# Hybrid attention layer on one core: group A in rounds of two query tiles, later va projections, a fixed order for ScalarE's counts and evictions

## The chip, the core and the metric

The kernel runs as one program on one core of a Trainium2 chip. The metric is the device time of one execution in microseconds (us). Before the change the median of three runs is 1526.25 us (1521.85 to 1529.15).

## The reference

One decoder layer for 1024 tokens of width 1024, batch 1, in float32:

```
h    = rmsnorm(x) * (1 + sc1) + sh1            # sh1, sc1, ga1, sh2, sc2, ga2: silu(c) @ w_ada + b_ada
proj = h @ w_in  ->  qa, ka, va, qb, ckv, qi, ki, wi
out_a = dilated_mixture(qa, ka, va)            # 8 heads of 64, windows (128,1), (512,4), (2048,16)
score[t, s] = sum_h wi[t, h] * relu(qi[t, h] . ki[s])    # 8 index heads, causal
idx   = top_k(score, 256)                      # per query
out_b = softmax attention over the picked rows of the latent ckv (8 heads)
x = x + ga1 * (concat(out_a, out_b) @ w_out)
x = x + ga2 * ((silu(gate) * up) @ w_down)     # gate, up = modulated rmsnorm(x) @ w_gu
return rmsnorm(x)
```

In group A a query sees the keys of its own and of the preceding 128-token tile (near), and keys at strides of 4 and 16 (far). The three branches are merged by their softmax denominators.

## The kernel before

The layer runs as a row of stages: the first norm, the index projections and the index scores (to about 193 us of the profiled execution), the projections beside the top-k search (193 to 410), attention of group A (410 to 551), attention of group B (551 to 705), the output projection, the feed-forward part and the last norm. Products that must be exact in float32 are three matmuls of high and low halves (L367 to L369 for 128x512 or 128x256 results, L377 for the near scores of a head).

Each engine runs its queue in order, and that queue is put in order by a scheduler when the program is built; `tc.issue_after(x)` adds a rule to it, that what is issued inside stands behind x on its engine. SP, ACT and POOL issue DMAs, in the order of their queues too.

Modulation (`modulation`, L328 on) is eight steps, one for each half of sc2, sh2, ga1 and ga2. A step loads 2 MB of w_ada in four DMAs into a ring of three places that lies in the tile `va` (L339), has eight matmuls (L342), a copy into `sm` on ScalarE (L343) and a second small product (L347 or L351). All eight are written ahead of the first index scores (`mod(8)`, L473).

The projections are a Python generator (`projections`, L537). It has va first: two weight blocks of 8 results of 128x256 each, evicted by ScalarE (L518). Then come six weight blocks, two each of kind a (queries of group A), k (its keys) and b (queries of group B). A block is four results of 128x512; ScalarE evicts each (L499) and so frees its PSUM bank (there are five), GpSimd splits it into halves (L503, L504), and SP stores n32, nh and nl to DRAM (L506, L509). The weights come by SP (L209) and are split by GpSimd (L214, L215).

The top-k search (`chain`, L649) looks bit by bit for the 256th largest score of each of the query tiles 2 to 7. It is two searches of 16 steps. A step counts three tiles on VectorE (L626) and three on ScalarE (Sign with a sum, L629), then VectorE joins the counts (L632, L634) to the next threshold. Between the searches VectorE builds a second key (L645 to L659). The loop at L674 on interleaves both: each `yield` of the chain allows so many units of projection (1.3 a step), a 128x512 result is two units, a 128x256 result one. A step of the chain stands behind the last eviction issued (`issue_after(ev.ins)`).

After the searches `pick` (L695) turns the thresholds of a tile into a mask, on VectorE alone; tiles 7, 6 and 5 ahead of group A, tiles 2 and 3 in its second head pair, tile 4 in its third. `table` (L721, L722) builds a bias table from `tab`, which an ACT DMA loads (L548).

Group A (`attend_a`, L867) has four head pairs, each with two halves of four query tiles. For every tile and head: near scores (three matmuls, L377), far scores (L891, eight small matmuls for the two heads), VectorE adds the bias and takes the row minimum (L896), ScalarE takes the exponential (L898), TensorE transposes (L910), ScalarE and VectorE evict (L920, L922), TensorE multiplies by the values (L935, and L946 for the far blocks at the end of a half). PSUM has four banks for scores, three for transposes, one for outputs. `staged(..., 0, 0)` (L993) writes the tiles one after the other, and the scheduler interleaves TensorE's instructions. The far operands q32 and k32 are loaded for every head pair (L972, L973).

## Time and profile before

| | us |
|---|---|
| median of three runs | 1526.25 |
| profiled execution | 1529.23 |
| its span in the trace | 1527.5 |
| index stage ends, projections begin on TensorE | 193 |
| keys of the search ready on VectorE | 208 |
| first search step's counts complete | 240.8 |
| group A begins on VectorE | 410.4 |
| group B begins | 551.4 |

The tables of lines give busy time and the mean of one instruction, then the idle time of the engine just ahead of it and what ended it. The chain of waits is followed back from the last instruction of the program.

### The profile page before, as it was taken

What the parts mean: (1) busy time and instruction counts of PE and PEld (TensorE: products, weight loads), DVE (VectorE), ACT (ScalarE), POOL (GpSimd) and SP (SyncE); (2) the same over time, 40 slices, a digit from 0 to 9 for tenths busy, and PEclk for the clock granted to TensorE, in tenths of its full rate; (3) what the DMA queues carried; (4) which work ended last, traced back from release to release, by engine and by line L of the source; (5) the groups of instructions that cost most, each with busy time, mean ns of one, the idle gap of its engine ahead of it and who ended that gap; (6) DMA issues with size and microseconds to landing.
All of it is one profiled execution on the core that took longest, in us unless ns stands there. A gap on an engine that the chain in (4) does not pass through costs nothing.

```text
span 1527.5 us, 20498 instructions
## 1 busy us (share of the span) xinstructions
PE 1369.7 (90%) x7477; PEld 1065.3 (70%) x7477; DVE 1042.7 (68%) x1808; ACT 602.9 (39%) x1211; POOL 618.5 (40%) x412
## 2 busy tenths in 40 slices
PE   0899999999499989998995999999999999888894
PEld 0666589877266657777883888888888887676773
DVE  5845756999856446664499854455545558999997
ACT  2425425556244455652265433333333332332334
POOL 3540214545200023001146654444444534677865
PEclk9999999999678989999996999999999999999998
DMA  9634544445723122125352322222222255313003
GB/s 251 198 99 136 179 121 129 145 124 165 221 91 132 43 84 70 43 70 154 116 166 84 110 83 83 83 83 83 83 84 79 85 186 208 104 63 124 21 0 111
DMA packets 139264, 171.53 MB, mean 112 GB/s; under 512 B 10197, under 2 KB 96022, under 8 KB 137626
## 3 DMA queue, kind: packets, MB, share of 16 engines
q1 hardware_dynamic: 131312, 142.67, 30.7%
q0 software_dynamic: 5984, 24.65, 4.7%
q10 hardware_dynamic: 1866, 2.90, 0.6%
q8 instruction: 59, 0.97, 0.3%
q14 instruction: 43, 0.35, 0.1%
HBM read 124.56 MB, written 45.09 MB: 111 GB/s over the span
## 4 chain that ended last, share of the span: by engine, by line
PE 61%; DVE 24%; DMA 5%; POOL 4%; issue 3%; ACT 2%; SPq 1%; DVEq 0%; POOLq 0%; ACTq 0%
DVE score L626 6%; PE mm L377 6%; PE mm L1213 5%; PE mm L1215 5%; PE mm L1214 5%; PE mm L367 4%; PE mm L368 4%; PE mm L369 4%; PE o L817 3%; PE tp L765 3%; PE tp L1213 3%; PE tp L1215 3%; PE tp L1214 3%; DVE yacc L1333 2%; DVE wo L1323 2%
## 5 line engine op out<-in xcount | busy, mean ns | idle before, releaser
L1197 ACT ACTIVATE wo<-f 128x512 fp32r<-128x512 f32 x124 | 77.8, 630 | 176.4 <-PE mm L1215 78.4
L1198 DVE TENSOR_TENSOR wo<-f,wo 128x512 fp32r<-128x512 f32 x124 | 107.5, 869 | 42.8 <-ACT wo L1197 41.0
L367 PE MATMUL mm<-hh,wl 128*128 128x512 f32 (+2 forms) x288 | 112.1, 390 | 5.9 <-ACT n L499 4.6
L368 PE MATMUL mm<-hh,wh 128*128 128x512 f32 (+2 forms) x288 | 110.2, 383 | 0.0
L369 PE MATMUL mm<-hl,wh 128*128 128x512 f32 (+2 forms) x288 | 108.6, 386 | 0.0
L367 PE MATMUL mm<-wo,wo 128*128 128x512 f32 x148 | 60.1, 406 | 10.3 <-DVE wo L1323 10.3
L367 PEld LDWEIGHTS mm<-hh,wl 128*128 128x128 f32 (+1 forms) x288 | 54.5, 189 | 19.7 <-ACT n L499 5.4
L1010 POOL TENSOR_TENSOR wor<-wor,ga 128x1024 f32<-128x1024 f32 x8 | 18.9, 2371 | 114.0 <-DMA wor<-in_w_out_dram 114.0
L215 POOL TENSOR_TENSOR wl<-wraw,wh 128x1024 fp32r<-128x1024 f32 (+1 forms) x22 | 53.1, 2430 | 24.1 <-ACT wh L212 24.0
L368 PEld LDWEIGHTS mm<-hh,wh 128*128 128x128 f32 (+1 forms) x288 | 54.6, 189 | 11.4 <-issue 0.8
L369 PEld LDWEIGHTS mm<-hl,wh 128*128 128x128 f32 (+1 forms) x288 | 53.2, 188 | 12.8 <-issue 1.7
L377 PE MATMUL mm<-wl,wh 64*128 64x256 f32 (+1 forms) x192 | 38.5, 351 | 24.1 <-DVE mn L896 24.0
L369 PE MATMUL mm<-wo,wo 128*128 128x512 f32 x148 | 58.1, 402 | 1.6 <-DVE wo L1323 1.6
L753 ACT ACTIVATE ttB<-ttB,mn 128x128 f32<-128x128 f32 (+7 forms) x64 | 49.3, 771 | 25.7 <-DVE mn L748 25.4
L368 PE MATMUL mm<-wo,wo 128*128 128x512 f32 x148 | 59.2, 400 | 0.0
L1323 DVE TENSOR_TENSOR wo<-f,wo 128x1536 fp32r<-128x1536 f32 (+1 forms) x17 | 56.3, 3317 | 0.6 <-ACT wo L1322 0.6
L367 PE MATMUL mm<-wo,ml 128*128 128x512 f32 x128 | 52.0, 406 | 4.5 <-DVE ml L1074 4.5
L426 DVE SCALAR_TENSOR_TENSOR score<-rl,wi,score 128x384 f32<-128x384 f32 (+2 forms) x70 | 49.8, 750 | 8.2 <-ACT rl L420 5.6
L765 PE MATMUL tp<-ident,ttB 128*128 128x128 f32 x288 | 50.2, 297 | 4.2 <-ACT ptB L768 4.2
L898 ACT ACTIVATE ttA<-ttA,mn 128x320 f32<-128x320 f32 (+4 forms) x64 | 36.3, 569 | 40.8 <-DVE mn L896 39.6
L626 DVE TENSOR_SCALAR_CACHE_REDUCE score<-ka,sc 128x768 bf16<-128x768 int16 (+2 forms) x48 | 52.3, 1140 | 0.0
L626 DVE TENSOR_SCALAR_CACHE_REDUCE score<-kl,sc 128x1024 bf16<-128x1024 uint16 (+2 forms) x48 | 52.3, 1139 | 0.0
(446 smaller groups left out, 4298.6 us busy)
## 6 DMA issues: line engine op xcount, KB each, us to landing
f<-in_w_gu_dram SPq DMA_DIRECT2D x44, 512.0 KB, 4.0
va<-in_w_ada_dram SPq DMA_DIRECT2D x32, 512.0 KB, 4.6
spg<-f POOLq DMA_DIRECT2D x44, 256.0 KB, 2.8
wraw<-in_w_in_dram SPq DMA_DIRECT2D x21, 512.0 KB, 5.2
f<-spg SPq DMA_DIRECT2D x33, 256.0 KB, 3.0
f<-in_w_down_dram SPq DMA_DIRECT2D x23, 256.0 KB, 3.6
more<-in_w_down_dram SPq DMA_DIRECT2D x21, 256.0 KB, 5.1
xi<-in_x_dram SPq DMA_DIRECT2D x8, 512.0 KB, 8.6
```

What stands on the lines that cost most here:

```text
L367: PE.matmul(p, al, bh, start=(j == 0), stop=False)
L368: PE.matmul(p, ah, bh, start=False, stop=False)
L369: PE.matmul(p, ah, bl, start=False, stop=(j == n - 1))
L377: PE.matmul(ps_[e], q[r, qs], k[r, ks], start=(i == 0), stop=(i == 2))
L626: V.tensor_scalar(mask(t, u), keys[:, seg[t]], z[:, i:i + 1], 0.0, op0=OP.is_lt, op1=OP.add, accum_out=cnt[:, i:i + 1])
L765: PE.transpose(pb[:, (k - k0) * P:(k - k0 + 1) * P], pe[:, k * P:(k + 1) * P], ident)
L1197: A.activation(h_, src, AF.Copy)
L1198: V.tensor_tensor(l_, src, h_.bitcast(F32), op=OP.subtract)
L1213: PE.matmul(p, w[1][:, k], a[0][:, k], start=(k == 0), stop=False)
L1214: PE.matmul(p, w[0][:, k], a[0][:, k], start=False, stop=False)
L1215: PE.matmul(p, w[0][:, k], a[1][:, k], start=False, stop=(k == 3))
L1323: V.tensor_tensor(l_, x, h_.bitcast(F32), op=OP.subtract)
```

## The change

1. Modulation: four of the eight steps stand ahead of the index scores, and one each with the first four blocks of the projections. `sm` moves to a pool that lives longer.
2. The projections take the blocks in the order a, a, k, k, v, v, b, b. The load of `tab` moves from the first block to the fifth, behind the va weights.
3. `signed[0]` is the last count on ScalarE; evictions of the projections are issued behind it, and counts behind the eviction, so that ScalarE has one fixed order. The shares of the loop change (3.0 for 3.5 units at the start, 4.8 for 4.0 between the searches, 0.75 more for some results of the first four blocks).
4. Tile 4's pick moves ahead of group A; tile 2's is done in its second head pair, tile 3's in its third.
5. Group A runs in rounds of two query tiles. Every TensorE operation goes through `on_pe`, which puts it behind the one before, so that TensorE has the order in which the code is written. `staged(..., 1, 2)` has the transposes one round behind the scores and the values two. `tts` has eight buffers instead of four.

```diff
-    mod(8)
+    mod(4)
...
+    todo = [(kind, base + i * 256, i) for kind, base in (("a", C_QA), ("k", C_KA), ("v", C_VA), ("b", C_QB))
+            for i in range(2)]
...
-        for e in range(2):
-            yield from proj_va(e)
...
+            if i < 4:
+                mod(1)
+            if i == 4:
                 with tc.issue_after(lastw[0].ins):
                     A.dma_start(tab, lnm.rearrange("u p n -> p u n"))
...
-    made, due, ev = 0, 3.5, None
+    made, due, ev = 0, 3.0, None
+
+    def behind(ins):
+        return tc.issue_after(ins.ins) if ins else nullcontext()
...
-            ev, n = next(work)
+            with behind(signed[0]):
+                ev, n = next(work)
             made += n
-        with tc.issue_after(ev.ins):
+        with behind(ev):
             dt = next(steps, None)
...
-    for pk in picks[:NV]:
+    for pk in picks[:3] + picks[5:]:
...
+    pe_last = [None]
+
+    def on_pe(op, *args, **kw):
+
+        with tc.issue_after(pe_last[0].ins) if pe_last[0] else nullcontext():
+            pe_last[0] = op(*args, **kw)
...
+            for u in range(2):
+                for i, (a, b) in enumerate(((1, 0), (0, 0), (0, 1))):
+                    for e in range(2):
+                        r = slice(e * HD, (e + 1) * HD)
+                        on_pe(PE.matmul, pps[u][e][:, nf:], q[r, a, ts[u]], kk[r, b, ks[u]],
+                              start=(i == 0), stop=(i == 2))
...
-    staged([it for p in range(4) for it in attend_a(p, va, pre_a)], 0, 0)
+    staged([it for p in range(4) for it in attend_a(p, va, pre_a)], 1, 2)
```

On ScalarE, at the first counts of the search, the order before is this. L518 is the eviction of a va result, L629 a count.

```order
L518 ACTIVATE va_95<-mm_2058 128x256
L518 ACTIVATE va_95<-mm_2084 128x256
L629 ACTIVATE score_94,sc_1816<-ka_1654,sc_1814 128x384
L518 ACTIVATE va_95<-mm_2122 128x256
L629 ACTIVATE score_94,sc_1816<-ka_1654,sc_1814 128x512
L629 ACTIVATE score_94,sc_1816<-ka_1654,sc_1814 128x640
L518 ACTIVATE va_95<-mm_2160 128x256
L629 ACTIVATE score_94,sc_1854<-ka_1654,sc_1826 128x384
```

Now, on the same engine at the same place, L499 is the eviction of a block of kind a and L634 a count:

```order
L499 ACTIVATE n32_1690<-mm_1665 128x512
L499 ACTIVATE n32_1724<-mm_1699 128x512
L634 ACTIVATE score_94,sc_1733<-ka_1576,sc_1731 128x384
L634 ACTIVATE score_94,sc_1733<-ka_1576,sc_1731 128x512
L634 ACTIVATE score_94,sc_1733<-ka_1576,sc_1731 128x640
L634 ACTIVATE score_94,sc_1745<-ka_1576,sc_1743 128x384
L634 ACTIVATE score_94,sc_1745<-ka_1576,sc_1743 128x512
L634 ACTIVATE score_94,sc_1745<-ka_1576,sc_1743 128x640
L499 ACTIVATE n32_1784<-mm_1759 128x512
```

Ahead of the first count there stood fourteen va evictions, and one among the counts of the step; now there are two evictions of kind a, and then one after every two steps.

On VectorE, between the last key (L582) and the first count (L626), the order before has the bias table of the first head (L721, L722), which reads `tab`:

```order
L582 TENSOR_TENSOR ka_1654<-ka_1654,cap_73 128x128
L721 SCALAR_TENSOR_TENSOR bt0_3443<-tab_96 128x2x192
L722 SCALAR_TENSOR_TENSOR bt0_3443<-tab_96 128x2x256
L582 TENSOR_TENSOR ka_1654<-ka_1654,cap_73 128x128
L608 COPY tp_1698<-lim0_1685 128x6
L626 TENSOR_SCALAR score_94,sc_1816<-ka_1654,sc_1814 128x768
```

Now that table (L732, L733) stands in the eighth step of the second search, between its counts (L631) and their joining (L637):

```order
L631 TENSOR_SCALAR score_94,sc_2634<-kl_1577,sc_2595 128x1024
L631 TENSOR_SCALAR score_94,sc_2634<-kl_1577,sc_2595 128x896
L631 TENSOR_SCALAR score_94,sc_2634<-kl_1577,sc_2595 128x768
L732 SCALAR_TENSOR_TENSOR bt0_3443<-tab_96 128x2x192
L733 SCALAR_TENSOR_TENSOR bt0_3443<-tab_96 128x2x256
L637 TENSOR_TENSOR sc_2642<-sc_2634,tp_1620 128x6
```

The table has moved out of the way of the first count and into the middle of the second search, two instructions in both.

On TensorE, in the first half of group A's first head pair, the order before changes between the kinds of work every few instructions. L377 are near scores, L891 far scores, L910 transposes, L935 values:

```order
L935 MATMUL o<-ptA_3485,va 64x128
L910 MATMUL tp<-ident,ttA_3481 64x128
L377 MATMUL mm<-wl,wh 128x256 x2
L891 MATMUL mm<-k_3489,q_3488 32x128 x2
L910 MATMUL tp<-ident,ttA_3482 128x128 x2
L910 MATMUL tp<-ident,ttA_3482 64x128
L891 MATMUL mm<-k_3489,q_3488 32x128 x4
L377 MATMUL mm<-wl,wh 128x256 x3
L935 MATMUL o<-ptA_3484,va 64x128
L910 MATMUL tp<-ident,ttA_3483 128x128 x2
```

Now it reads thus, every row under the helper's line L883; the names say the kind (mm near or far scores, tp transposes, o values):

```order
L883 MATMUL mm<-wl,wh 128x256 x12
L883 MATMUL mm<-k_3501,q_3500 32x192 x16
L883 MATMUL tp<-ident,ttA_3488 128x128 x3
L883 MATMUL tp<-ident,ttA_3489 128x128 x3
L883 MATMUL tp<-ident,ttA_3490 128x128 x3
L883 MATMUL tp<-ident,ttA_3491 128x128 x3
L883 MATMUL o<-ptA_3496,va 64x128
L883 MATMUL o<-ptA_3497,va 64x128
L883 MATMUL o<-ptA_3496,va 64x128
L883 MATMUL o<-ptA_3497,va 64x128
```

A round now has the twelve near matmuls of two tiles and two heads together, then the sixteen far ones, then the transposes of the round before, then the values of the round before that.

Of the modulation, the first six steps stand in the index stage in both orders; the steps for ga2 move from among the va results to among the results of kind k. On SP the fourth load of the seventh step now stands behind the store of a half of the seventh result of kind a, the third of the eighth step behind the store of the first result of kind k, and the fourth behind that of the fourth. From the second head pair of group B to the end the orders of all engines are the same.

## Rows read from the trace of the kernel before

**Rows 1.** The page: busy time by engine, and shares of the ending chain.

```profile
PE 1369.7 (90%) x7477; PEld 1065.3 (70%) x7477; DVE 1042.7 (68%) x1808; ACT 602.9 (39%) x1211; POOL 618.5 (40%) x412
...
PE 61%; DVE 24%; DMA 5%; POOL 4%; issue 3%; ACT 2%; SPq 1%; DVEq 0%; POOLq 0%; ACTq 0%
```

**Rows 2.** Windows: busy us (count) of PE, PEld, DVE, ACT, POOL; clock, DMA share, GB/s.

```profile
376.00:395.00 19.00, 11.99 (x61) 9.60 (x60) 19.00 (x22) 7.28 (x11) 11.61 (x8) 0.88 0.89 284
395.00:410.00 15.00, 0.00 (x0) 0.00 (x0) 15.00 (x19) 0.00 (x0) 2.18 (x3) 0.50 1.01 265
410.00:425.00 15.00, 14.26 (x76) 8.34 (x76) 5.83 (x23) 5.45 (x20) 0.00 (x0) 0.50 0.12 43
425.00:440.00 15.00, 15.00 (x127) 9.15 (x126) 6.19 (x19) 5.19 (x15) 0.54 (x1) 0.68 0.05 19
...
515.00:530.00 15.00, 15.00 (x168) 9.96 (x168) 6.66 (x25) 7.02 (x24) 0.00 (x0) 1.00 0.05 19
410.00:551.40 141.40, 137.81 (x1253) 91.73 (x1253) 78.85 (x241) 64.71 (x197) 1.61 (x3) 0.83 0.22 78
```

**Rows 3.** Timeline of VectorE at the start of the search: start, duration, line, idle before.

```profile
207.85 0.22 DVE L582 TENSOR_TENSOR ka<-ka,cap 128x128 int16<-128x128 int16 x1
...
222.90 0.56 DVE L721 SCALAR_TENSOR_TENSOR bt<-tab 128x384 f32<-128x384 f32 x1 [14.82 <-DMA tab<-in_lnm_dram]
...
240.78 0.16 DVE L632 TENSOR_TENSOR sc<-sc,tp 128x6 f32<-128x6 f32 x1 [12.39 <-ACT score L629]
```

**Rows 4.** Timeline of VectorE between the searches, and at their end.

```profile
298.95 1.02 DVE L637 TENSOR_SCALAR v<-sc 128x6 f32<-128x6 f32 x1
...
312.78 1.26 DVE L626 TENSOR_SCALAR_CACHE_REDUCE score<-kl,sc 128x1024 bf16<-128x1024 uint16 x1
...
380.67 1.18 DVE L702 TENSOR_SCALAR kl<-kl,v 128x1024 uint16<-128x1024 uint16 x3
...
409.33 0.55 DVE L721 SCALAR_TENSOR_TENSOR bt<-tab 128x384 f32<-128x384 f32 x1
```

**Rows 5.** Timeline of ScalarE, a step of the first search and an eviction.

```profile
248.93 0.62 ACT L629 ACTIVATE score<-ka,sc 128x384 bf16<-128x384 int16 x1 [1.05 <-DVE sc L634]
...
255.20 0.58 ACT L499 ACTIVATE n<-mm 128x512 f32<-128x512 f32 x1
```

**Rows 6.** TensorE lines, 193 to 390: busy us, mean ns, idle before.

```profile
L367 PE MATMUL mm<-hh,wl 128*128 128x512 f32 x192 | 76.0, 396 | 5.9 <-ACT n L499 4.6 <-POOL wl L215 1.3
```

**Rows 7.** DMA issues, 193 to 300, then 375 to 452: KB each, median us to landing.

```profile
va<-in_w_ada_dram SPq DMA_DIRECT2D x5, 512.0 KB, 5.7
...
q<-spna ACTq DMA_DIRECT2D x2, 384.0 KB, 4.3
k<-spnk SPq DMA_DIRECT2D x2, 384.0 KB, 9.5
```

**Rows 8.** Chain of waits in group A: start, length, what.

```profile
410.74 1.01 PE mm L377 x3
...
440.83 7.42 DMA q<-spna
448.38 0.47 PE mm L891 x16
...
478.38 1.53 DVE ka L703
...
510.93 0.57 PE mm L377 x6
511.50 0.59 PE tp L910 x4
...
513.62 0.55 PE mm L377 x3
...
515.21 0.59 PE o L935 x8
515.80 1.64 PE o L946 x32
```

More of the change, by code (lines that the diff above doesn't have):

```diff
@@ L609, in hybrid_block @@
     picks = []
+    signed = [None]
     def column():
@@ L684, in hybrid_block @@
         due += dt
-    for _ in work:
-        pass
+    with behind(signed[0]):
+        for _ in work:
+            pass
     natc.close()
@@ L924, in values @@
-        def values(half, i):
-            t = half * 4 + i
-            k0 = max(0, t - 1)
-            if i == 0:
+                        o = (2 * d + u - 2) * P + 32 * r
+                        on_pe(PE.matmul, pps[u][e][rs_, :nf], q32[kr_, o:o + 32],
+                              kfar[kr_, :nf // 32, rs_], start=True, stop=True)
+            for u in range(2):
+                for e, pp in enumerate(pps[u]):
+                    n = pp.shape[1]
+                    tt = tts[4 * (d % 2) + 2 * u + e]
+                    mn = small.tile([P, 2], F32, name="mn", tag="mn", bufs=8)
+                    V.tensor_tensor_reduce(tt[:, :n], pp, (bt[e] if p or e else bt0)[:, 1 - u, NB - n:], scale=-1.0,
+                                           scalar=3.0e38, op0=OP.add, op1=OP.min, accum_out=mn[:, 0:1])
+                    A.activation(tt[:, :n], tt[:, :n], AF.Exp, bias=mn[:, 0:1], scale=-1.0,
+                                 accum_out=st["lt", half][:, i0 + u, e:e + 1])
@@ L928, in values @@
+        def values(d):
+            half, i0 = d // 2, 2 * (d % 2)
+            if i0 == 0:
                 st["o", half] = mm_tile("o")
@@ L945, in values @@
                         h = 2 * p + e
-                        PE.matmul(pov[e * HD:(e + 1) * HD, i0:, rs_], vc[:kk, b, r, h * HD:(h + 1) * HD],
-                                  far[e][:, :, rs_], start=False, stop=(b == 0 and r == 3))
+                        on_pe(PE.matmul, pov[e * HD:(e + 1) * HD, c0:, rs_], vc[:kk, b, r, h * HD:(h + 1) * HD],
+                              far[e][:, :, rs_], start=False, stop=(b == half and r == 3))
             fin(p, half, po, st["lt", half])
-        return [tuple((lambda f=f, a=half, b=i: f(a, b)) for f in (scores, turn, values))
-                for half in range(2) for i in range(4)]
+        return [tuple((lambda f=f, d=d: f(d)) for f in (scores, turn, values)) for d in range(4)]
     banks(4, 3, 1)
@@ L985, in pre_a @@
             with tc.issue_after(last.ins):
-                for pk in picks[NV:5] if p == 1 else picks[5:]:
-                    pick(*pk)
+                pick(*picks[2 + p])
         if p == 3:
```

113 lines of the change are left out of this document (52 added, 61 removed).

## The prediction

> **What bounds the kernel now.** I read the page's totals first: TensorE is busy for 90% of the span and holds 61% of the ending chain, VectorE holds 24% [rows 1]. So time can come from two places: where TensorE has nothing to do, and where its clock is low. The windows show both around the start of group A. From 395 to 410 us TensorE has no instruction at all while VectorE is busy throughout; the next 15 us run at a granted clock of 0.50, the 15 after those at 0.68, against 1.00 from 515 to 530 [rows 2]. The whole stretch of group A, 410 to 551.4, has a mean of 0.83.
>
> Why does VectorE come late? Its own timeline tells. The keys are ready at 207.85 + 0.22 = 208.1. Then it waits 14.82 us for the table's load, and 12.39 us at the joining of the first step for ScalarE's counts [rows 3]. Those counts stand behind va evictions on ScalarE, as the order shows; va evictions wait for TensorE. From 240.78 to 298.95 lie fifteen further steps and 0.39 us, so 3.85 us a step, bound by VectorE: ScalarE's three counts start at 248.93 and the next eviction, which is behind a further step's counts, comes at 255.20, which leaves it idle time in each step [rows 5]. The end of the first search to the start of the second is 13.8 us, the second search and its closing counts 67.9 us, three picks 28.7 us [rows 4]. VectorE begins group A at 410.4, the time at which TensorE begins again.
>
> **The search and the picks.** The va evictions go from ScalarE's way, the table from VectorE's. The two evictions that now stand ahead of the counts belong to results that TensorE makes from 193 on. TensorE ends the projections at 376 + 11.99 = 388 [rows 2]; less 5.9 of waits [rows 6] that is 189 us for 24 results of 128x512 and 16 of half their size, 32 in all, and two modulation steps: at most 5.9 us a result. Both are done by about 205, before the keys. So the first step starts at 208.1. In before its equivalent start is 240.98 - 3.85 = 237.1, hence 29 us are gained. Forward: 208.1 + 16 x 3.85 = 269.7; + 13.8 = 283.5; + 67.9 = 351.4; + 1.25 for the table that now lies in the second search (0.56 and 0.69) = 352.7. Tile 4's pick comes on top ahead of group A: 28.7 us for widths of 1024, 896 and 768 is 10.7 ns a column, times 640 is 6.8. Picks end at 352.7 + 35.5 = 388, 21 us earlier than 409.3.
>
> Where could the chain wait for TensorE? A step allows 1.3 units, a result of at most 5.9 us is two, so a step asks for at most 3.8 us of TensorE in 3.85: TensorE keeps its lead, and its five banks let it run up to five results beyond ScalarE. The table's load is issued behind a count about 4.8 us ahead of its reader and needs about 3.4; I count no wait, and up to 5 us if it shares the engines with weights.
>
> **TensorE's projections.** Its work from 193 to 388 stays the same instructions in another order: 195 us, of which 5.9 are waits [rows 6]. Added are the waits of the last two modulation steps. The seventh step's fourth load stands on SP behind a store of the seventh result. ScalarE evicts two results ahead of the counts and then one every two steps, so the seventh behind the counts of step ten, 208.1 + 9 x 3.85 + 2.3 = 245; with the split on GpSimd (about 1) and 5.7 us of load [rows 7] it lands about 252. TensorE needs it behind the eight results of kind a and a piece of the next, at about 243 by at most 5.9 us each: 9 us. For the eighth step the same count gives 4 us around 290. If all of the old waits remain the end is 388 + 13 = 401, if they go 395; bounds for the added waits are 0 (the loads in time) and 2 x 10. I take 395 less 1, since the old ones were for evictions that now come sooner: 394. These 13 us are behind five banks of results, so the chain feels them only if it has used up that lead; that is a rival below.
>
> So group A begins at about 394 (TensorE later than VectorE's 388) and not at 410.4: 16 us.
>
> **Group A.** In before it takes 551.4 - 410.4 = 141 us. The work of TensorE at full clock I sum from the chain. Six near matmuls beside one another, three of each head, take 0.57 us, three of one head alone 0.55 [rows 8]: two heads next to each other cost no more than one. In the order before many stand alone; now all are alternated. 192 near matmuls / 6 x 0.57 = 18.2. Far scores: 384 / 16 x 0.47 = 11.3. Transposes: 184 / 4 x 0.59 = 27. Values: 240 / 8 x 0.59 = 17.7. Far values: 192 / 32 x 1.64 = 9.8. 32 transposes of the finishing 4.7. The prologue of group B's matmuls there, 36 of 128x512 at 5.25 / 24 us, 7.9. Sum 97 us. VectorE has 78.85 us of work there less tile 4's pick (6.8), ScalarE 64.7 [rows 2]: both are below it. Over this floor I put 5 us for the first far scores, which wait for q32 and k32 (4.3 and 9.5 us from issue [rows 7], issued near 388 to 393, while the near scores of two tiles take 2.5), and for sixteen rounds about 0.6 us each, 9 us, for transposes whose third bank comes free only with an eviction. 97 + 14 = 111 us. Group A then ends at 394 + 111 = 505.
>
> Where do the other 30 us go? The second head pair's wait for q32, 7.42 us, is on the chain now, and so is tile 4's pick, whose first instruction stands there at 478.38 [rows 8], 6.8 us; the low clock after the empty stretch accounts for 15 x (1 - 0.50) + 15 x (1 - 0.68) = 12 us of the first thirty alone [rows 2]. The last 4 are left for the pairing of heads.
>
> The idle stretch of TensorE before group A, 388 to 410.7, is followed by clock 0.50; the 7.42 us for q32 at 440 is far shorter. Behind group A's start I count no idle stretch beyond 6 us now, so full clock. The Trainium skill, page "TensorE: Matmul & The Clock Gate", section "A second HAM failure mode: psum-queue depth-cycling", speaks against this: groups of matmuls that cycle through PSUM banks with small idle times between can make the clock oscillate. No stretch of before tests rounds that wait on four score banks; windows without an idle time, as 515 to 530, have 1.00, in agreement so far. By that rule the gain in group A would shrink to the rivals three and four, which are priced from rows.
>
> From group B's second head pair on the order is the same on every engine, so what is gained by then is a shift to the end. Sum: 551.4 - 505 = 46 us off the profiled execution's 1529.2, so 1483. That execution lies 3 us above the median and inside the runs' 1521.85 to 1529.15 to within 0.1.
>
> **The rivals.** Two: the chain waits for TensorE. If no lead is left when the w_ada loads come late, the 13 us go into both the search and TensorE: picks end at 401, group A begins at 402, TensorE has by then stood idle for some us and runs its first ones at the lower clock, another 6. 505 + 8 + 6 = 519, the time 1497. For it: ScalarE's order is now fixed both ways, a late result stops the counts. Against it: the five banks.
>
> Three: rounds in a fixed order wait. TensorE can no longer fill a wait for VectorE with other tiles' work. Each of sixteen rounds then pays a latency of scores, minimum, exponential, transposes: 141 us as before for group A, starting at 394, ends at 535, the time 1513; half of that, 1498. For it: VectorE's 72 us and its picks fall in lumps. Against it: scores, transposes and values are from three different rounds.
>
> Four, slower: the waits of the rounds keep the clock at its lower level (1.2 in place of 2.4 GHz). Three near matmuls took 1.01 us at 0.50 and 0.55 at full [rows 8], a factor of 1.84; the 97 us become 178, with 14 of waits 192, from 394 to 586: 35 us later than before, 1564. It decides for slower once group A takes over 157 us, which is about 1.4 times my figure. [...] For it: 0.50 for 15 us although TensorE was busy for 14.26 of them [rows 2]. Against it: the clock went up by itself to 0.68 and beyond in the same stage.
>
> Five: the moved modulation also shortens the index stage, or group A needs only its floor of 97: 1469 to 1473. The order speaks against the first, since the first six steps stay there.
>
> **How the numbers follow.** The forecast, 1483, has 0.58; two 0.13; three 0.17 (spread from 1495 to 1515); four 0.04; five 0.08. The forecast's own range is 1473 to 1495: starts between 388 and 401, group A between 103 and 118. The range for 8 in 10 takes in five's upper half, two and most of three: 1467 to 1509. A change of less than 0.5% can't be told from none by these runs; around the median that is 1518.6 to 1533.9. Faster: 0.91; within: 0.05 (three at its worst, with late loads on top); slower: 0.04.
>
> **What would show it.** VectorE's waits of 14.8 and 12.4 us at the start of the search are gone and the first count starts near 208; the picks end near 388; TensorE waits about 9 us near 245 for w_ada; the clock in the first thirty us of group A is above 0.9; group B begins near 505, and every later stage has its old length. It is wrong if group A takes over 125 us, if VectorE's step is longer than 3.85 us for waits on ScalarE, or if the shift is given back behind group B.

## Result: 1474.6 us, and the profile of the changed kernel

| | before | after |
|---|---|---|
| median (range) of the runs compared, us | 1524.05 (1512.84 to 1529.15) | 1474.62 (1472.60 to 1487.49) |
| ratio, 95% interval | | 0.9703 [0.9624, 0.9782] |
| profiled execution, span, us | 1527.5 | 1471.0 |
| first minimum of group A on VectorE | 410.4 | 395.1 |
| first minimum of group B | 552.2 | 509.0 |
| last minimum of group B | 691.2 | 640.3 |
| end of the span | 1527.5 | 1471.0 |

The change takes about 3% off. The forecast was 1483 with 1467 to 1509 around it: right in sign and within 10 us, and on the low side of the gain. The last four lines of the table split the 56.5 us between the two profiled spans: group A starts 15.3 us earlier, is 27.9 us shorter (141.8 before, 113.9 after), group B is 7.7 us shorter (139.0, 131.3), and 5.6 us come behind it. The spans are of one execution each; the medians lie 49.4 us apart, so some of the 56.5 is chance (the last part of the explanation says which).

The page of after (answers to [rows 1]): TensorE has lost 53 us of busy time with the same 7477 instructions, VectorE has gained 9. A gain of busy time without a lost instruction is the first hint that not only waits went.

```profile
PE 1316.7 (90%) x7477; PEld 1040.1 (71%) x7477; DVE 1051.7 (72%) x1808; ACT 599.7 (41%) x1211; POOL 629.0 (43%) x412
```

Here is the search on VectorE in the timeline of after (start, duration, engine, line, operation, idle before). It answers to [rows 3, 4].

```profile
206.34 2.17 DVE L583 SCALAR_TENSOR_TENSOR ka<-kr,score 128x896 int16<-128x896 int16 x1
...
212.65 1.00 DVE L631 TENSOR_SCALAR_CACHE_REDUCE score<-ka,sc 128x768 bf16<-128x768 int16 x1
...
216.11 0.16 DVE L637 TENSOR_TENSOR sc<-sc,tp 128x6 f32<-128x6 f32 x1
...
231.72 0.16 DVE L637 TENSOR_TENSOR sc<-sc,tp 128x6 f32<-128x6 f32 x1
...
235.57 0.16 DVE L637 TENSOR_TENSOR sc<-sc,tp 128x6 f32<-128x6 f32 x1
...
274.49 1.02 DVE L642 TENSOR_SCALAR v<-sc 128x6 f32<-128x6 f32 x1
...
359.28 1.17 DVE L713 TENSOR_SCALAR kl<-kl,v 128x1024 uint16<-128x1024 uint16 x3
...
394.05 0.55 DVE L732 SCALAR_TENSOR_TENSOR bt<-tab 128x384 f32<-128x384 f32 x1
...
395.33 1.41 DVE L732 SCALAR_TENSOR_TENSOR bt<-tab 128x384 f32<-128x384 f32 x1
```

The reader is to see: the first count at 212.65, the first joining (L637) at 216.11 with no wait printed behind it, where before it had 12.39 us; the 14.82 us in front of the table are gone; two joinings 3.85 us apart; and the picks' end at 394.05.

The start of group A on TensorE's timeline of after:

```profile
393.09 0.96 PE L883 MATMUL mm<-wl,wh 64*128 64x128 f32 x12
395.47 0.38 PE L883 MATMUL mm<-wl,wh 64*128 64x256 f32 x1 [1.42 <-DVE mn L920]
398.67 1.70 PE L883 MATMUL mm<-wl,wh 64*128 64x256 f32 x11 [2.83 <-DVE mn L920]
407.90 0.68 PE L883 MATMUL mm<-k,q 64*32 64x64 f32 x32 [7.53 <-DMA k<-spnk]
```

It then waits 1.42 and 2.83 us for VectorE and 7.53 for k32. Group A of after in windows, which answer to [rows 2] (busy us and count of PE, PEld, DVE, ACT, POOL; clock, DMA share, GB/s):

```profile
405.00:420.00 15.00, 10.60 (x155) 7.78 (x155) 6.65 (x27) 6.19 (x22) 0.54 (x1) 0.63 0.80 224
420.00:435.00 15.00, 13.11 (x150) 10.50 (x149) 13.02 (x40) 8.41 (x27) 0.00 (x0) 0.77 0.55 211
435.00:450.00 15.00, 12.99 (x220) 10.32 (x216) 11.40 (x36) 9.66 (x31) 0.53 (x1) 1.00 0.38 144
...
395.10:509.00 113.90, 92.14 (x1258) 72.33 (x1258) 75.08 (x235) 65.94 (x202) 7.77 (x10) 0.90 0.44 144
```

TensorE goes from the projections straight into group A (393.1), where before it had nothing from 395 to 410, and the clock is low until 435. The last row is the key one. The same stretch of before, from its first minimum of group A to that of group B, reads in the view of windows:

```profile
410.40:552.20 141.80, 138.36 (x1258) 92.14 (x1258) 79.08 (x243) 65.40 (x199) 2.03 (x4) 0.83 0.22 77
```

The same 1258 instructions: 138.4 us of busy time before, 92.1 after. So group A is shorter by 27.9 us because its matmuls take 46.2 us less, while the time in which TensorE has nothing to do has grown from 3.4 to 21.8. The mean granted clock rose from 0.83 to 0.90; at 0.90 the work of before would be 138.4 x 0.83 / 0.90 = 128 us (an estimate from these two rows), so about 11 of the 46 us can be the clock and 35 are something else.

### The profile page after: what moved, and what is told of

Read it like the earlier page. It is cut to its first block, busy times and chain, and to the rows that moved or that the text cites. A ratio compares the mean times of both kernels' runs of the same rounds, so it can differ in the third digit from the quotient of the medians.

```text
span 1471.0 us, 20493 instructions
## 1 busy us (share of the span) xinstructions
PE 1316.7 (90%) x7477; PEld 1040.1 (71%) x7477; DVE 1051.7 (72%) x1808; ACT 599.7 (41%) x1211; POOL 629.0 (43%) x412
## 4 chain that ended last, share of the span: by engine, by line
PE 46%; DVE 12%; POOL 5%; issue 3%; DMA 3%; ACT 1%; SPq 1%; POOLq 0%; DVEq 0%; ACTq 0%
PE mm L1236 5%; PE mm L1238 5%; PE mm L1237 5%; PE o L828 3%; PE mm L378 3%; PE tp L1236 3%; PE tp L1237 3%; PE tp L776 3%; PE tp L1238 3%; DVE yacc L1356 3%; DVE wo L1346 2%; PE o L883 1%; PE o L1236 1%; PE o L1238 1%; PE o L1237 1%
## 5 line engine op out<-in xcount | busy, mean ns | idle before, releaser
L1221 DVE TENSOR_TENSOR wo<-f,wo 128x512 fp32r<-128x512 f32 x124 | 106.6, 862 | 42.4 <-ACT wo L1220 40.5
L368 PE MATMUL mm<-hh,wl 128*128 128x512 f32 (+2 forms) x288 | 112.5, 392 | 0.1
L216 POOL TENSOR_TENSOR wl<-wraw,wh 128x1024 fp32r<-128x1024 f32 (+1 forms) x22 | 53.3, 2438 | 23.8 <-ACT wh L213 23.7
L504 POOL TENSOR_TENSOR nl<-n,nh 128x512 fp32r<-128x512 f32 x24 | 45.8, 1912 | 17.0 <-ACT nh L501 8.8
L631 DVE TENSOR_SCALAR_CACHE_REDUCE score<-ka,sc 128x768 bf16<-128x768 int16 (+2 forms) x48 | 52.3, 1140 | 0.0
L631 DVE TENSOR_SCALAR_CACHE_REDUCE score<-kl,sc 128x1024 bf16<-128x1024 uint16 (+2 forms) x48 | 52.3, 1140 | 0.0
L1290 POOL TENSOR_TENSOR f<-f 128x512 f32<-128x512 f32 x15 | 19.8, 1322 | 74.9 <-ACT f L1289 74.9
L369 PE MATMUL mm<-wo,mh 128*128 128x512 f32 x128 | 50.4, 394 | 0.0
```

The costliest lines, as they stand in the source:

```text
L216: G.tensor_tensor(lo, raw, hi.bitcast(F32), op=OP.subtract)
L368: PE.matmul(p, al, bh, start=(j == 0), stop=False)
L369: PE.matmul(p, ah, bh, start=False, stop=False)
L631: V.tensor_scalar(mask(t, u), keys[:, seg[t]], z[:, i:i + 1], 0.0, op0=OP.is_lt, op1=OP.add, accum_out=cnt[:, i:i + 1])
L1221: V.tensor_tensor(l_, src, h_.bitcast(F32), op=OP.subtract)
```

## Experiments

Each kernel is the changed one with one edit, or before with one part of the change. "Group A" and the like are measured between the same landmarks as above. Before had 1520.6 us (median) on the chip of the first four, 1522.2 on that of the second four, 1525.9 on that of the last four.

| kernel | us (range) | ratio to before, 95% | group A start, length | group B starts |
|---|---|---|---|---|
| front only | 1502.66 (1499.05 to 1511.31, once 1524.43) | 0.9842 [0.9773, 0.9911] | 392.3, 141.5 | 533.8 |
| group A only | 1483.08 (1476.10 to 1487.85) | 0.9719 [0.9655, 0.9782] | 410.6, 109.2 | 519.8 |
| unpaired | 1468.25 (1466.92 to 1473.48) | 0.9632 [0.9573, 0.9690] | 392.5, 112.0 | 504.5 |
| far loads | 1482.77 (1477.14 to 1491.23) | 0.9725 [0.9655, 0.9795] | 393.4, 118.3 | 511.7 |
| heads apart | 1486.31 (1485.13 to 1489.63) | 0.9774 [0.9700, 0.9849] | 391.4, 125.7 | 517.1 |
| free order on TensorE | 1486.00 (1480.81 to 1491.54) | 0.9767 [0.9700, 0.9833] | 393.5, 125.9 | 519.4 |
| va first | 1474.26 (1465.53 to 1484.51) | 0.9692 [0.9615, 0.9768] | 398.9, 109.1 | 508.0 |
| far loads 2 | 1473.93 (1468.75 to 1478.47) | 0.9686 [0.9618, 0.9753] | 393.7, 115.5 | 509.2 |
| after again | 1473.43 (1470.67 to 1476.20) | 0.9650 [0.9612, 0.9688] | 394.9, 112.5 | 507.4 |
| combined | 1470.13 (1467.99 to 1473.31) | 0.9632 [0.9593, 0.9670] | 392.7, 109.8 | 502.5 |
| ScalarE's order | 1506.00 (1496.13 to 1515.89) | 0.9863 [0.9804, 0.9922] | 397.8, 138.6 | 536.4 |
| pick back | 1469.92 (1468.21 to 1473.29) | 0.9623 [0.9568, 0.9677] | 392.8, 113.3 | 506.1 |

**The change in two halves.** Front only has all of the change but group A, which is as in before (single tiles, no fixed order):

```
-        def scores(d):
+        def scores(half, i):
...
-    staged([it for p in range(4) for it in attend_a(p, va, pre_a)], 1, 2)
+    staged([it for p in range(4) for it in attend_a(p, va, pre_a)], 0, 0)
```

> The changed kernel with group A as it was before (single tiles, the scheduler's order of TensorE, four row buffers): only the order of the projections, of the modulation, of ScalarE and of the picks is new. Theory (the two parts add: 15 us are won ahead of group A, 28 us by the rounds in it, 13 us behind it follow from how group A ends): group A begins near 395 and lasts 120 to 130 us, as its waits are partly gone (tile 4's pick) but two heads stand apart again; 1492 to 1503 us. Rival (group A became short because no idle stretch lies ahead of it and the pick is gone, the rounds add nothing): group A lasts 105 to 115 us, 1470 to 1480 us.

Group A only is the reverse: before, with the changed `attend_a` and its staging alone.

```
-    mod(4)
+    mod(8)
...
-        with behind(ev):
+        with tc.issue_after(ev.ins):
...
-    for pk in picks[:3] + picks[5:]:
+    for pk in picks[:NV]:
```

> The kernel before with group A alone in rounds of two tiles, TensorE in the written order, eight row buffers; projections, search and picks as before. Theory: group A begins at 410 with the low clock as before, lasts about 118 us (111 and tile 4's pick), and the 7 us at the boundary to group B are won here too: 1493 to 1503 us. Rival (rounds add nothing, or without the earlier picks TensorE waits in its fixed order for the pick): group A lasts 130 us or more, 1510 to 1527 us.

The halves add up: 17.9 and 37.5 us off before, 55.4 together; the whole took 52.4 off on the last chip and 49.4 on the first. Both recorded theories missed in group A: front only was to last 120 to 130 us there, group A only about 118. Front only starts group A 18 us earlier, without tile 4's pick in it and with 3.9 us of wait for k32 in place of the 7.42 for q32, and group A still lasts 141.5 us. So moving the pick and halving the load's wait did not shorten it. The window of front only:

```profile
392.30:533.80 141.50, 133.60 (x1258) 87.90 (x1258) 75.94 (x235) 68.76 (x202) 7.69 (x10) 0.86 0.34 114
```

and that of group A only:

```profile
410.60:519.80 109.20, 92.53 (x1258) 72.36 (x1258) 78.03 (x243) 63.57 (x199) 2.13 (x4) 0.91 0.31 105
410.60:425.60 15.00, 12.48 (x126) 9.26 (x128) 8.21 (x35) 8.16 (x30) 0.00 (x0) 0.50 0.23 60
425.60:440.60 15.00, 9.02 (x122) 6.97 (x122) 13.77 (x36) 6.77 (x22) 0.54 (x1) 0.96 0.55 211
```

Without the new order TensorE is busy for 133.6 us, with it for 92.5, whichever front goes ahead. Group A only comes out of the same empty stretch as before and has the same 0.50 in its first 15 us, but 0.96 in the next 15, where before had 0.68 [rows 2]. Front only, with the earlier start alone, has 0.52, 0.50 and 0.61 in its first three stretches of 15 us. So what the clock gave back came with the rounds and not with the earlier start.

**Which part of the order?** Three kernels change only the order of TensorE's matmuls within the rounds. Unpaired lets the three matmuls of a head follow one another; head 1's three still stand directly behind head 0's:

```
-                for i, (a, b) in enumerate(((1, 0), (0, 0), (0, 1))):
-                    for e in range(2):
+                for e in range(2):
+                    for i, (a, b) in enumerate(((1, 0), (0, 0), (0, 1))):
```

> The changed kernel, but the three near matmuls of one head stand ahead of the three of the other in place of alternating; the rest is the same, the same matmuls. Theory (two heads beside one another cost no more than one: 0.57 us for six, 0.55 for three): 64 times 0.55 in place of 32 times 0.57, 17 us more in group A, less what lies beside VectorE's work: 1480 to 1492 us. Rival (TensorE's order within a round is of no account): within 3 us of the changed kernel, 1472 to 1478 us.

The recorded theory, 17 us more in group A, did not come: group A lasts 112.0 us.

Heads apart puts all of head 0's scores of a round (both tiles, near and far) ahead of head 1's:

```
-            for u in range(2):
-                for i, (a, b) in enumerate(((1, 0), (0, 0), (0, 1))):
-                    for e in range(2):
+            for e in range(2):
+                for u in range(2):
+                    for i, (a, b) in enumerate(((1, 0), (0, 0), (0, 1))):
```

> The changed kernel, but in a round all near and far matmuls of the first head stand ahead of all those of the second; the same matmuls. After the run in which the three near matmuls of a head stood ahead of the other's three cost nothing. Theory (matmuls of the two heads run at the same time on two halves of the array as long as they stand close in the queue; what shortened group A is that equal kinds of both heads now stand together): twelve near matmuls take 2.2 us in place of 1.0, the far ones somewhat more, 16 rounds, so 15 to 20 us more in group A: 1486 to 1496 us. Rival (group A became short because fewer changes between kinds of work stand in the queue, the heads do not matter): 1472 to 1479 us.

Free order on TensorE keeps the rounds, their buffers and their staging, and lets the scheduler order the matmuls:

```
-        with tc.issue_after(pe_last[0].ins) if pe_last[0] else nullcontext():
-            pe_last[0] = op(*args, **kw)
+        op(*args, **kw)
```

> The changed kernel without the fixed order on TensorE in group A: the rounds of two tiles, the stages and the eight row buffers stay, the scheduler orders. In its order the near matmuls of the later rounds stand in threes and sixes of one head, but values and far ones in whole blocks. Theory (equal kinds of both heads side by side are what counts; this order keeps a good part): group A 115 to 122 us, 1474 to 1484 us. Rival (the fixed order itself is needed): group A 130 us or more, 1490 us or more.

Here is the busy time of group A's lines on TensorE, by kind, from the profile's groups. The kinds overlap one another at their edges and smaller kinds are left out, so a column doesn't add up to TensorE's busy time, which is the fifth row.

| us busy | before | front only | after | unpaired | heads apart | free order |
|---|---|---|---|---|---|---|
| near scores, x180 | 37.6 | 35.0 | 17.7 | 18.2 | 30.1 | 28.0 |
| far scores, x384 | 22.5 | 23.0 | 8.7 | 8.7 | 16.7 | 15.4 |
| values, x240 | 31.4 | 30.3 | 17.5 | 17.3 | 16.9 | 23.7 |
| transposes, x184 | 35.0 | 35.5 | 29.0 | 28.9 | 28.9 | 32.5 |
| TensorE in group A | 138.4 | 133.6 | 92.1 | 91.5 | 109.1 | 113.4 |
| its mean granted clock | 0.83 | 0.86 | 0.90 | 0.91 | 0.90 | 0.89 |

The last four columns have nearly the same clock, so what differs among them is not the clock. The windows of heads apart and of free order:

```profile
391.40:517.10 125.70, 109.06 (x1258) 84.79 (x1258) 75.28 (x235) 67.74 (x202) 7.75 (x10) 0.90 0.40 130
```

```profile
393.50:519.40 125.90, 113.42 (x1258) 80.62 (x1258) 74.71 (x235) 67.23 (x202) 7.72 (x10) 0.89 0.39 129
```

The rows behind two of these columns (line, operation, tiles, shapes, count; busy us, mean ns of one, idle before), of before:

```profile
L377 PE MATMUL mm<-wl,wh 64*128 64x256 f32 (+1 forms) x180 | 37.6, 355 | 24.1 <-DVE mn L896 24.0
...
L935 PE MATMUL o<-ptA,va 128*64 128x128 f32 x240 | 31.4, 325 | 0.0
L891 PE MATMUL mm<-k,q 64*32 64x128 f32 (+2 forms) x384 | 22.5, 319 | 1.3 <-DMA q<-spna 1.3
```

and of after:

```profile
L883 PE MATMUL tp<-ident,ttA 128*128 128x128 f32 (+1 forms) x184 | 29.0, 297 | 8.8 <-ACT ptF L944 3.0 <-DVE ptA L946 2.3 <-ACT ptA L944 1.9
L883 PE MATMUL mm<-wl,wh 64*128 64x256 f32 (+1 forms) x180 | 17.7, 324 | 4.7 <-DVE mn L920 4.2 <-DVE kB L875 0.5
L883 PE MATMUL o<-ptA,va 128*64 128x128 f32 x240 | 17.5, 289 | 0.0
L883 PE MATMUL mm<-k,q 64*32 64x128 f32 (+2 forms) x384 | 8.7, 294 | 7.5 <-DMA k<-spnk 7.5
```

The mean of one instruction hardly falls (355 to 324 ns for the near scores) while the busy time halves: the group's instructions lie over one another. (The 24.1 us of idle time in before lie mostly ahead of the window; the span from the projections' end is counted there.) One round shows it plainly on TensorE's timeline of after:

```profile
442.18 0.98 PE L883 MATMUL mm<-wl,wh 64*128 64x256 f32 x12
443.09 0.88 PE L883 MATMUL mm<-k,q 64*32 64x192 f32 x32
```

and on that of heads apart:

```profile
443.11 0.97 PE L883 MATMUL mm<-wl,wh 64*128 64x256 f32 x6
444.01 0.85 PE L883 MATMUL mm<-k,q 64*32 64x192 f32 x16
```

Twelve near matmuls of two heads take 0.98 us, six of one head alone 0.97; 32 far ones 0.88, 16 of one head 0.85. A head's 64 channels are half of the array's rows, the other head has the other half, and the two run beside each other when they are near enough in the queue. Unpaired shows how near: triple behind triple is as good as one by one. Heads apart is 12.4 us slower than far loads 2 (below), which ran on the same chip and has the time of after; free order is 12.1 slower, between the ranges of its two recorded theories. The rival of heads apart, that fewer changes between kinds of work shortened group A, would have left it at 1472 to 1479 us. So the order alone is worth about 12 us in time. Heads apart undoes the pairing of the scores only, and that is 17 of the 46 us of busy time. The rest of group A's gain is left to the rounds: free order, which has them without the fixed order, needs 113.4 us of TensorE against 133.6 of front only, with 28.0 against 35.0 for the near scores. That this too is pairing is likely; no run takes the rounds apart.

**The first far scores.** After has 7.5 us of wait for k32. Far loads moves the last head pair's spill stores from SP to GpSimd's queue and q32's first load from ScalarE's to SP's:

```
-            q = G if last and half else nc.sync
+            q = G if last else nc.sync
...
-        A.dma_start(q32, spill_n["a"][p, :, 2 * P:])
+        (nc.sync if p == 0 else A).dma_start(q32, spill_n["a"][p, :, 2 * P:])
```

> The changed kernel, but the last two results of kind b are all stored by GpSimd's queue, and q32 of the first head pair is loaded by SP, so that the loads of q32 and k32 stand no longer behind stores and evictions that wait for GpSimd. Theory (the 7.5 us that TensorE waits for k32, and the low clock of 0.63 and 0.77 from 405 to 435, come from that queue order): k32 is issued near 394 in place of 398.3, TensorE's wait falls to 2 to 4 us, 1462 to 1470 us. Rival (the loads share the DMA engines with 1 MB loads and land no sooner, or the stores on GpSimd's queue come in the way): 1471 to 1478 us.

The wait falls to 2.0 us, and another comes: the first finishing on VectorE writes into memory that the late store still reads. The chain of far loads (start, length, what) has it:

```profile
400.19 11.00 DMA spqb<-nl
...
411.37 0.43 DVE mxA L793
```

and TensorE's waits from 390 to 425 (what waited for what: us in total, times, longest) show who pays:

```profile
PE tp L883 <- ACT ptF L944: 6.7, 1, 6.7
...
PE mm L883 <- DMA k<-spnk: 2.0, 1, 2.0
```

TensorE waits 6.7 us one round later for what stands behind that finishing. Group A is not shorter for it (118.3). Two of its four executions took 1477 to 1478 us and two 1488 to 1491. The profiled one, of the longer two, also has a longer group B (143.1 us); a window of it shows the clock low although TensorE is busy:

```profile
508.00:548.00 40.00, 39.08 (x183) 25.27 (x179) 18.32 (x57) 17.12 (x42) 12.40 (x7) 0.66 0.28 92
```

What lowers it there stays open, and with it how much of far loads' loss is its own doing. Far loads 2 splits the stores over three queues, so that none lies behind two others:

```
-            q = G if last and half else nc.sync
...
+                q = G if last and half else A if last and u else nc.sync
```

> As the run with the earlier far loads, but the stores of the last results stay where they were, save one on ScalarE's queue, so that no store lands late. Theory (the 7.5 us wait for k32 was only traded for the wait of the first finishing for a late store, whose buffer it takes): k32 is issued near 394, TensorE waits for it 2 to 4 us, no wait of 5 us or more takes its place, 1464 to 1471 us. Rival (the DMA engines are full between 395 and 411 and something there is always late): 1472 us or more, with another wait of 4 us or more in the first 25 us of group A.

Here TensorE waits 2.6 us for k32 and 3.3 for an eviction (ptF) in its place, and the time is that of after (1473.9 and 1473.4), not the 1464 to 1471 of the theory. The wait can be traded, and the trade brings nothing that these runs can tell.

**The front.** The kernel "ScalarE's order" is before with an edit of the fixed order of ScalarE's counts and evictions alone: va stays first, the modulation stays ahead, picks and group A as in before. One thing more moves by itself: the scheduler puts the bias table, which in before stood ahead of VectorE's first count, behind several search steps (its first row starts at 264.8).

```
-                    A.activation(mask(t, u), keys[:, seg[t]], AF.Sign, bias=z[:, i:i + 1], scale=-1.0,
-                                 accum_out=cnt[:, i:i + 1])
+                    signed[0] = A.activation(mask(t, u), keys[:, seg[t]], AF.Sign, bias=z[:, i:i + 1], scale=-1.0,
+                                             accum_out=cnt[:, i:i + 1])
...
-            ev, n = next(work)
+            with behind(signed[0]):
+                ev, n = next(work)
```

> The kernel before with the fixed order of ScalarE alone: counts behind the eviction, evictions behind the last count; va first, modulation ahead, table load, picks and group A as before. ScalarE then has four va evictions and the two last modulation steps ahead of the first count, not fourteen evictions. Theory (the row of evictions in the way is what delayed the search, the table's load the smaller part): the first count of ScalarE near 226 in place of 236, the search step after it 10 to 13 us earlier, group A begins at 398 to 402: 1509 to 1516 us. Rival (the scheduler's order was only a sign of something else that is late): the picks end within 4 us of 409, 1519 to 1526 us.

The first joining of this kernel on VectorE's timeline:

```profile
226.50 0.16 DVE L633 TENSOR_TENSOR sc<-sc,tp 128x6 f32<-128x6 f32 x1 [16.12 <-ACT score L630]
```

and, from ScalarE's timeline of before, what stood ahead of its first count:

```profile
233.09 0.38 ACT L518 ACTIVATE va<-mm 128x256 f32<-128x256 f32 x1 [2.50 <-PE mm L369]
235.97 0.38 ACT L518 ACTIVATE va<-mm 128x256 f32<-128x256 f32 x1 [2.50 <-PE mm L369]
236.26 0.61 ACT L629 ACTIVATE score<-ka,sc 128x384 bf16<-128x384 int16 x1
```

In before the counts stand behind va evictions, which come only every 2.9 us, as TensorE makes them. With the order fixed the joining comes at 226.50 in place of 240.78, 14.3 us earlier, and group A starts 12.6 us earlier (397.8). Up to about 2 of the 14.3 are the table's move: VectorE's own part of the step ended at 228.4 in before, behind the table, and at 210.4 here, so with the table in its old place the joining could not have come before 228.4. The whole front gives 18.1 at group A's start (392.3). So most of the front's gain is that ScalarE's queue no longer holds evictions in front of counts. The rest of it (the modulation behind, the table's load later, the results' order) is worth some 5 us at group A's start; in time the two kernels can't be told apart (ratios 0.9863 and 0.9842, with intervals that overlap).

Va first has the changed kernel's results in the order va, q, k, b:

```
-    todo = [(kind, base + i * 256, i) for kind, base in (("a", C_QA), ("k", C_KA), ("v", C_VA), ("b", C_QB))
+    todo = [(kind, base + i * 256, i) for kind, base in (("v", C_VA), ("a", C_QA), ("k", C_KA), ("b", C_QB))
```

Here later modulation weights land in the tile va over some of its results, so its values lack those; the instructions are the same.

> The changed kernel with the va results first again, as in before; the two later steps of the modulation, the fixed order of ScalarE, the picks and group A as changed. Theory (the search starts early because ScalarE's counts no longer queue behind a long row of evictions, by the fixed order and the smaller start share; which results come first is of no account): the first count of ScalarE near 213, the picks end near 394, 1470 to 1479 us. Rival (va first brings the old wait back): the picks end 15 to 25 us later, 1485 to 1495 us.

Group A starts 4 us later than in after again and group B within 0.6; the time is the same. Which results come first is of no account for the time as long as ScalarE's order is fixed.

Pick back takes tile 4's pick back into group A:

```
-    for pk in picks[:3] + picks[5:]:
+    for pk in picks[:3]:
...
-                pick(*picks[2 + p])
+                for pk in picks[3:5] if p == 1 else picks[5:]:
+                    pick(*pk)
```

> The changed kernel with tile 4's pick back in the third head pair of group A and the picks of tiles 2 and 3 in the second, as before. Theory (the picks end 7 us earlier, but TensorE ends its projections only at 393 and then waits for k32, so nothing is won ahead; in group A TensorE is the busier engine and the pick costs little there): within 4 us of the changed kernel. Rival (the pick on VectorE holds TensorE in its fixed order, as it did on the chain before): 6 to 10 us slower.

It makes no loss: 1469.9 against 1473.4 of after again, with ranges that overlap.

**A repeat and a sum.** After again is the changed kernel, unchanged, for the chip of the last four. Combined puts unpaired and far loads 2 together.

> The changed kernel itself once more, as the measure for the others of this call: 1470 to 1480 us, a ratio to before of 0.963 to 0.976.

> The changed kernel with both variants that were not slower: the three near matmuls of a head ahead of the other's three, and the far loads no longer behind the last stores. Theory (group A is bound by TensorE only in part; the wait for k32 is 5 us shorter, some of it comes back as waits for evictions): 1464 to 1472 us, 3 to 6 us below the changed kernel. Rival (all of it comes back): within 2 us of the changed kernel.

Combined is 3.3 us below after again, pick back 3.5, and on other chips unpaired is lower too; their ranges overlap with after's. A version that is better by 0.2% is possible, not shown.

## Why the prediction was right, and where its sum was not

**Right: the two waits at the search's start.** Both are gone, the step is still 3.85 us, and no wait of the chain for TensorE or the table appears. Rival two fell with that. The start itself, 212.65, is 4.5 us later than the 208.1 that I took: I had the keys end as before, but GpSimd now works beside VectorE's building of them. One 896-wide step took 2.17 us at 206.34, beside a split, and 1.08 in before, when GpSimd had no work; the steps that are longer beside splits make up about 3 us, a row beside another GpSimd instruction 1. Then 274.49 to 359.28 is 84.8 us where [rows 4] had 81.7. Of the difference 1.25 is the table, as forecast, and the other 1.7 lies in one row between the searches (L663, 6.62 us in place of 4.88). The picks took 34.8 us (35.5 forecast). So they end at 394, not 388, and group A starts at 395.1, not 394, because now VectorE is last and not TensorE. Six us of error on VectorE cost one us of the start, since the forecast had TensorE as the later.

**Right: TensorE's end of the projections**, 393.1 against 394, by waits of another make than I named. In the table of waits of after, from 193 to 395:

```profile
PE o L352 <- ACT sm L344: 4.9, 1, 4.9
PE o L348 <- DMA sm<-in_b_ada_dram: 3.3, 2, 2.0
PE o L343 <- DMA va<-in_w_ada_dram: 2.0, 1, 2.0
```

I forecast 9 and 4 us for the weights w_ada. They cost 2.0; 8.2 come from the modulation's tile `sm`, filled by ScalarE's eviction and by a load of its own. The sum is 10.2 in place of 13.

**The step that failed: where group A's 30 us go.** Its length was forecast as 111 us and was 113.9 (112.5 in after again). The sum of durations [rows 8] was sound in the main: 97 us of busy time forecast, 92.1 measured. (One of its terms, 5.25 us for 24 matmuls of the prologue, stands in no row; at the 0.23 us each that the chain of before shows, its 7.9 us would be 8.3.) The waits were 14 us in the sum and 21.8 measured, so that the length came out so near is in part luck. The account of the difference to before was wrong. I gave 7.4 us to the wait for q32, 6.8 to the pick, 12 to the low clock and what was left, 4, to the pairing of heads. Front only has the earlier start, no such pick and half the load's wait, and gained nothing in group A; group A only has the same clock of 0.50 in its first 15 us and gained 32.6. The term of the pairing was the mis-sized one: 4 us in the sum. About 35 us of busy time came with the rounds by the estimate above, and 17 of them go with the pairing of the scores alone (heads apart). The clock's 12 were near the 11 of that estimate, though not for the reason given, the empty stretch; and 18 of these 46 us came back as new waits. The rows could have told: 180 near matmuls at six in 0.57 us are 17 us, and that line was busy for 37.6 in before. I used [rows 8] for the floor and did not hold it against the busy time of the same line in before.

Three near matmuls of one head took 0.55 us and six of two heads 0.57 [rows 8]; here six took 0.97 and twelve 0.98. The Trainium skill, page "TensorEngine Tiling (Array Packing)", section "Theoretical Speedup", gives up to a factor of two where a dimension of the matmul is at most 64. The rows agree, with 1.98 for the near scores (2 x 0.97 / 0.98). Heads apart adds that the two must stand close together in TensorE's queue.

**Wrong: the clock.** "Above 0.9 in the first thirty us" did not hold: 0.63 from 405 to 420 and 0.77 to 435. My count of waits had 5 us for the far scores; there were 1.4, 2.8 and 7.5 us one after another ahead of 408. It went up by itself to 1.00 from 435. The prediction also read that windows of before without an idle time have 1.00. That holds for 515 to 530 and not for others: 425 to 440 and 450 to 465 have TensorE busy throughout at 0.68 and 0.83, and 480 to 500 has 19.1 us of work in 20 at 0.65. Rival four, by which the rounds' own waits keep it low, is refuted by the window 435 to 450 of after: 2.0 us of it idle, at 1.00. The section of the Trainium skill that the prediction had for it (page "TensorE: Matmul & The Clock Gate", "A second HAM failure mode: psum-queue depth-cycling") would have the clock swing with such waits; that window does not show it. Rival three (rounds wait for a latency each) had some truth in size: 8.8 us ahead of transposes and 4.7 ahead of near scores, where I put 9.

**Wrong, in our favour: the pure shift behind group A.** I took everything from group B's second head pair on as a shift. In the profiled pair it is 13.3 us better. At the border the finishing of group A's last head pair was on the chain in before, with its store and reload; chain of before:

```profile
552.29 5.59 DMA spm<-mxA
...
557.94 2.86 DMA mr<-spm
```

and of after:

```profile
504.10 2.07 PE o L883 x40
506.17 0.43 PE mm L368
...
512.64 2.84 DMA mr<-spm
```

In after the last values of group A stand, by the fixed order, ahead of the last prologue matmuls of group B (506 to 508.4), so the finishing and its store (5.59 us in before) run beside these. The store is off the chain, only the reload is left. The granted clock differs too. The window behind the border of before:

```profile
552.00:570.00 18.00, 13.29 (x59) 8.70 (x60) 8.98 (x33) 7.97 (x25) 7.19 (x5) 0.75 0.50 162
```

and that of after:

```profile
507.80:526.80 19.00, 18.05 (x111) 11.46 (x111) 12.18 (x43) 12.08 (x32) 9.06 (x5) 1.00 0.43 150
```

The other traces tell the store and the clock apart. The first 20 us are counted from group B's first minimum:

| kernel | group B, us | clock in its first 20 us | TensorE without work there, us | store on the chain |
|---|---|---|---|---|
| before | 139.0 | 0.72 | 4.5 | yes |
| front only | 140.7 | 0.56 | 1.3 | yes |
| ScalarE's order | 136.2 | 0.70 | 4.1 | yes |
| free order on TensorE | 133.9 | 0.74 | 2.4 | yes |
| heads apart | 131.3 | 1.00 | 0.9 | yes |
| group A only | 131.2 | 1.00 | 0.8 | no |
| after | 131.3 | 1.00 | 0.9 | no |

The store's place does not decide the length: heads apart has it on its chain (5.71 us from 515.1, 2 us ahead of the first minimum) and the short group B. The length goes with the clock: every kernel with 1.00 there has 131.2 to 131.4 us, and far loads, with 0.70 and TensorE's order as in after, 143.1. In before 3.6 of the 7.7 us are waits of TensorE and the rest is longer busy time of the same matmuls. The gain comes with group A's rounds in their fixed order (front only lacks it, group A only has it). Why the clock stays high there was not tested.

The last 5.6 us arise behind group B and before 805 (from there both spans run 56.5 us apart), and they are chance as far as the traces show. From group B's last minimum to the first weight split of the next stage (L1198, L1221 in after) before takes 113.7 us and after 108.0. Unpaired and far loads 2, with the same order there as after, take 111.8 and 112.1, and ScalarE's order 108.5. The granted clock of the stretch is 1.00 wherever it takes 108.0 to 108.5, and 0.97 or 0.98 in the others.

The sum by landmarks: 1 us less at the start than forecast, 2 less in group A, 13 more behind it: 56.5 in place of 46. Without the chance at the end it is about 51, between the 49.4 and 52.4 of the medians.

## What to carry to other kernels

Before pricing a reordering of TensorE, hold the busy time of each line against count times the shortest time per instruction that the trace shows for it: matmuls on half of the array that stand alone cost as much as two beside each other, and a gap of a factor of two there is a term of its own, larger than most waits. An engine's queue that mixes counts on the chain with evictions that wait for TensorE should have its order fixed; that was worth 12 to 14 us at the search's start here. When a stage that was not touched gets shorter, hold its granted clock against its waits in several traces before giving the gain to a transfer that left the chain.

## What the runs showed of the hardware

First, some work of GpSimd and of VectorE takes longer side by side. One of GpSimd's splits `nl` of 128x512, on its timeline of before, while VectorE closes the second search:

```profile
370.21 1.29 POOL L504 TENSOR_TENSOR nl<-n,nh 128x512 fp32r<-128x512 f32 x1 [1.64 <-ACT nh L501]
```

and two of them in after, while VectorE does its picks:

```profile
383.78 14.08 POOL L504 TENSOR_TENSOR nl<-n,nh 128x512 fp32r<-128x512 f32 x2 [4.15 <-ACT nh L501]
```

One takes 1.29 us in the first, two take 14.08 in the second, and the first of these two alone 12.5. This is why the last spill is late and with it k32: SP issues its load at 398.30, behind stores that wait for these splits. In the other direction the table's row of VectorE took 1.41 us at 395.33 and 0.55 at 394.05. Both lie within the two splits, so the lengthening comes and goes; the key step at 206.34 (2.17 us beside a split, 1.08 in before without one) is the cleaner pair. That the two engines hold each other up is the likely reading; how much of the 14.08 is waiting was not measured by itself (spans on GpSimd are rough).

Second, the clock can be at 0.66 over 40 us in which TensorE is busy for 39.1 (far loads, above), and at 0.65 from 480 to 500 of before with 19.1 of 20 us busy. What TensorE did differently ahead of these was not found; group B of after had 1.00.
